# Four linear-attention heads whose instructions are queued one projection earlier in a hybrid block

## The chip, the cores and the metric

The kernel runs on one core of a Trainium2 chip. The metric is the device time of one execution in microseconds (us). Three runs of the kernel before the change gave 1381.58, 1382.93 and 1383.07 us; their median is 1382.93 us.

## The reference, cut to what matters

One encoder layer over 1024 tokens of width 1024, all in float32: a norm, one wide input projection, gated linear attention of four heads in both directions beside a pooling branch, a gated merge, and a feed-forward block. The change lies in the input projection and the attention:

```python
h = rmsnorm(x, norm_mix[l])
proj = h @ w_in[l]
q, k, v, r, lr_f, lr_b, u, g_a, g_b = jnp.split(proj, split_points, axis=-1)
log_a_f = jax.nn.log_sigmoid(lr_f @ w_decay_up_fwd[l] + b_decay_fwd[l]) / GATE_NORMALIZER
log_a_b = ...
o_fwd = gla_chunked(qh, kh, vh, af, include_diag=True)      # per head: 128 keys, 256 values
o_bwd = jnp.flip(gla_chunked(jnp.flip(qh, 2), ..., include_diag=False), 2)
o = o_fwd + o_bwd
o = o * lax.rsqrt(jnp.mean(o * o, axis=-1, keepdims=True) + EPS)
o = o.transpose(0, 2, 1, 3).reshape(bsz, length, GLA_VALUE_DIM) * gla_norm[l]
o = (o * jax.nn.silu(r)).astype(x.dtype)
...
# gla_chunked, per chunk n:  S_n = decay_n * S_(n-1) + k_n^T v_n ;  o_n = (masked q_n k_n^T) v_n + q_n S
```

## The kernel before, in words

Every float32 product is made of three fast ones: both factors are split into a high part (a cast on ScalarE, ACT) and a low part (a subtraction on VectorE, DVE, or GpSimd, POOL), and `mm3` multiplies high by high, low by high and high by low. Weights come from memory as `raw` and are split into `wh` and `wl`; four `raw` buffers serve all weights in turn.

TensorE (PE) runs one long row of these products, 512 wide (`ps`). Counted from the start, the stretch that matters is: Q and K of head 0 (products 136 to 224), values of heads 0 and 1 (to 320), Q and K of head 1 (320 to 416) and of head 2 (416 to 512), values of heads 2 and 3 (512 to 704, by tiles 7, 6, 5 ... 0 of 128 tokens), Q and K of head 3 (704 to 800), then eight tiles of the gate r, `j` = 0 to 7, 48 products each (800 to 1184). Tiles 0 to 2 of r (`BY = 3`) are only kept; from `j` = 3 on each half of a tile also goes through `gated`: Silu on ACT, transposes of the finished attention output on PE (`tp`), and a multiplication on DVE.

Everything else is woven into that row. `pump(dt)` runs after each `mm3`, and gives time to three lists: `pending` (splits of weights for later products), `aside` (`beside(...)`: sums of weight blocks on POOL (`wsum`, stored as `s_out`), and later sums of feature blocks on DVE, one job per `every` units), and `side`, a queue of generators that run one after the other. Each `attention` is such a generator, and `yield t` says how many units of the main row pass before its next piece. It only sets the order in which instructions are issued. Each engine executes its own instructions in that order and waits at each for its inputs.

The pieces of one attention are:
- four gate products `z`, then Abs, Exp and Ln on ACT (a table load lies before Ln, and another before the next Exp); between them the previous head's output is scaled by `normalize` (DVE), and `flush` stores it to memory (`o_out`, issued by SyncE, SP);
- four times: `decay` (scan on DVE), `exponentials` (ACT), `apply_decay` (`ke` on DVE, `qe` on POOL), and two key transposes `kp`, split into `kt`;
- the backward chain, chunks n = 7 to 1: a product `kv` on PE, the state `st` on DVE, and its scaled copies `sb` and `so` on ACT; the next `st` needs `so`;
- the scores `sc`, masked and split into `p`;
- the outputs `op`, n = 0 to 7, each from `p`, the values, `sb` and the forward state `sf`.

Values are kept by `keep_values`, as `vh` (ACT) and `vl` (DVE), a pair of each per tile of tokens for two heads. An attention fetches Q and K as arguments; before its chain it waits, by half a unit at a time, until the dictionary `v_heads` has its head's values, which is filled once all eight tiles are there.

Of the kernel before, what the change touches and what calls it, by code (L numbers as in the profile page):

```python
# [23 lines left out]
HEADS = 4  # L24
# [29 lines left out]
def kernel(  # L54
# [42 lines left out]
    def slot(dtype=F32, shape=(2, HALF), s="slot"):  # L97
        return slots.tile([P, *shape], dtype, tag="slot", name=name(s))
# [90 lines left out]
    def begin(gen, delay=0.0):  # L189
        side.append([gen, delay])  # L190
# [284 lines left out]
    split_pair_weight()  # L475
    for kp in range(2):
        transpose_tile(trs[kp], xn[1], 1, kp)
    pair_v = {}, {}

    def keep_values(vs, t, ps):  # L480
        for v in vs:
            if t // 4 not in v:
                v[t // 4] = slot(F32R, (4, DV), "vh"), slot(F32R, (4, DV), "vl")
        parts = [[part[:, t % 4, :] for part in v[t // 4]] for v in vs]
        halves = [ps[:, h * DV : (h + 1) * DV] for h in range(2)]
        for (hi, _), src in zip(parts, halves):
            nc.scalar.copy(hi, src)
        for (hi, lo), src in zip(parts, halves):
            nc.vector.tensor_tensor(lo, src, as_f32(hi), op=ALU.subtract)

    def pair_products(ts, before=None):
        banks = [bank(ps_mm) for _ in ts]
        for k in range(KT):
            if before:
                before(k)
            for ps, t in zip(banks, ts):
                mm3(ps[:, :], tokens(hT(k, t // 4), t), pair_w[k], k == 0, k == KT - 1)
        for ps, t in zip(banks, ts):
            keep_values(pair_v, t, ps)

    def first_steps(k):
        if k == 2:
# [204 lines left out]
    def prepare_beside(jobs, every, put=PUT, lag=1):  # L707
        aside.append([beside(chain(*jobs), every, put, lag), every])
# [5 lines left out]
            aside.pop(0)  # L714


    v_heads, o_heads, unscaled = {}, {}, []
    HOLD, SCORES = 4.4, 6

    class ValueWeights:  # L720
# [32 lines left out]
        def products(self):  # L753
            while pending:
                pending.pop(0)()
            vs, banks = ({}, {}), {}
            self.split()
            self.split()

            def steps(t, ks):  # L760
                if t not in banks:
                    banks[t] = bank(ps_mm)
                for k in ks:
                    if (t, k) == (0, 6):
                        prepare()
                        credit[0] = 1.0
                    at = self.ORDER.index(k)
                    mm3(banks[t][:, :], tokens(hT(k, t // 4), t), self.parts[k], at == 0, at == KT - 1)
                if ks[-1] == self.ORDER[-1]:
                    keep_values(vs, t, banks[t])  # L770

            early, late = self.ORDER[:6], self.ORDER[6:]
            for ks in (early, late):
                for t in (7, 6):
                    steps(t, ks)
            for t in reversed(range(NT - 2)):
                if t == 2:
                    fetch()
                steps(t, self.ORDER)
            return vs  # L780

    def project_qk(last=False):
        q = slot(s="q")
        k = slot(s="k")
        for dst, scale in ((q, DK**-0.5), (k, 1.0)):
            final = last and dst is k
            w = take(not final)
            if final:
                value_weights[0].splits(2)
            elif last:  # L790
                value_weights.append(ValueWeights())
            for half in range(2):
                ps = feature_major(w, hT, half)
                nc.scalar.activation(dst[:, half, :], ps[:, :], AF.Copy, scale=scale)
        return q, k

    def attention(h, q, k):


        qe, ke = {}, {}  # L800
# [59 lines left out]
        def apply_decay(half, d):  # L860
            if half not in ke:
                ke[half] = slot(s="ke")
            f, e_q, e_k = fac[half, d], qe[half], ke[half]
            f2 = f[:, :8].rearrange("p (n a) -> p n a", a=2)
            nc.vector.tensor_tensor(e_k[:, d, :], zs[half, d][:, :], k[:, half, :], op=ALU.mult)
            nc.gpsimd.tensor_tensor(e_q[:, d, :], e_q[:, d, :], q[:, half, :], op=ALU.mult)
            nc.gpsimd.tensor_tensor(f[:, 8:], f2[:, :, 0], f2[:, :, 1], op=ALU.mult)
# [20 lines left out]
        def advance(old, n, d, kt, dst, ends=False):  # L888

            kv = bank(ps_g, "kv")  # L890
            products(kv[:, :DV], tokens((kt[:, 0, :], kt[:, 1, :]), n), value(n))
            new = s1((DV,), "st")[:, :]
            after = factor(n, d, "after")
            if old is None:
                nc.vector.tensor_scalar(new, kv[:, :DV], after, None, op0=ALU.mult)
            else:
                nc.vector.scalar_tensor_tensor(
                    new, kv[:, :DV], after, old[:, :], op0=ALU.mult, op1=ALU.add
                )
            following = n + 1 if d == 0 else n - 1  # L900
            nc.scalar.activation(dst, new, AF.Copy, scale=factor(following, d, "before"))
            if ends:
                return None
            old = s1((DV,), "so")
            nc.scalar.activation(old[:, :], new, AF.Copy, scale=factor(following, d, "whole"))
            return old
# [17 lines left out]
        exponentials(1, 1)  # L924
        decay(0, 1)
        yield 2
        apply_decay(1, 1)
        yield HOLD - 2
        exponentials(0, 1)
# [10 lines left out]
        kts[0, 1] = transposed_keys(0, 1)  # L940
        exponentials(1, 0)
        yield 2.5
        while h not in v_heads:
            yield 0.5
        v = v_heads[h]

        def value(n):
            return tuple(part[:, n % 4, :] for part in v[n // 4])

        sb = [slot(shape=(4, DV), s="sb") for _ in range(2)]  # L950
        old = None
        for n in range(NT - 1, 0, -1):
            m = n - 1
            old = advance(old, n, 1, kts[n // 4, 1], sb[m // 4][:, m % 4, :], m == 0)
            if n == 7:
                apply_decay(1, 0)
            yield 1.2
            if n == 3:
                kts[0, 0] = transposed_keys(0, 0)
                yield 0.5  # L960
        p = scores(0)
        yield SCORES
        o = [slot(shape=(4, DV), s="o") for _ in range(2)]
        ms = vec(NT, "oms")
        old = sf = None
# [50 lines left out]
    def first_qk():  # L1016
        q, k = slot(s="q"), slot(s="k")
        low_rank(0)
        weights = [take()]
        for half in range(2):  # L1020
            if half:
                finish_side()
                low_rank(1)
                prepare()
            for n, (dst, scale) in enumerate(((q, DK**-0.5), (k, 1.0))):
                if n == len(weights):
                    weights.append(take(ahead=False))
                ps = feature_major(weights[n], hT, half)
                nc.scalar.activation(dst[:, half, :], ps[:, :], AF.Copy, scale=scale)
        return q, k  # L1030

    value_weights = []
    for h in range(HEADS):
        qk = project_qk(h == 2) if h else first_qk()
        begin(attention(h, *qk))
        if h == 0:
            for ts in ((7,), (6,), (5, 4)):
                pair_products(ts)
            v_heads.update(enumerate(pair_v))
            prepare_beside(map(branch_jobs, range(2)), 3.7)  # L1040
        if h == 2:
            v_heads.update(zip((2, 3), value_weights.pop().products()))
            prepare_beside(map(branch_jobs, range(2, 4)), 4)

    class Unit:
# [132 lines left out]
    for j in range(KT):  # L1178
        if 2 <= j <= 4:
            load_o(j - 2)  # L1180
        w = take()
        if j == 6:
            for _ in range(2):
                gunits[0].load()
        if j == 7:
            gates_ahead.step()
        if j < BY:
            whole_r = slot(s="r")
        for half in range(2):
            if j >= BY and not sums_begun and (j > BY or not side):  # L1190
                finish_side()
                finish_beside()
                prepare_beside([feature_jobs(0), feature_jobs(1)], 2.3)
                sums_begun = True
            ps = feature_major(w, hT, half)
            if half == 0:
                flush()
            if j < BY:
                nc.scalar.copy(whole_r[:, half, :], ps[:, :])
                raw_r.append((j, half, whole_r[:, half, :]))  # L1200
            else:
                put_by()
                gated(j, half, ps[:, :])
            if j == KT - 1 and half == 0:
                gates_ahead.step()
# [882 lines left out]
```

## Time and profile before

| what | value |
|---|---|
| median of three runs | 1382.93 us |
| the profiled execution | 1381.07 us, its span 1379.2 us |
| busy time of PE, DVE, ACT, POOL | 1366.3, 836.6, 642.4, 750.6 us |
| granted TensorE clock | 1.00 |

The span is the time from the first to the last recorded instruction; 1.9 us of the execution lie around it. Busy time of an engine counts its instructions and not its waits. In a timeline row stand the start, the duration, the engine, the source line, the operation and its tiles (`out<-in`), and in brackets the idle time before it and who ended that. A row of the waits gives the total, the number and the longest.

### The profile page before, as it was taken

Reading aid. Unit: us, or ns where it says so; the run is one execution under the profiler, and the core shown is the slowest. Engines: PE = TensorE matmul, PEld = TensorE weight load, DVE = VectorE, ACT = ScalarE, POOL = GpSimd, SP = SyncE. Lnnn points to the kernel's source line nnn. Section 1 sums busy time; section 2 is a strip of 40 time slices with the busy share of each in tenths; the row PEclk is TensorE's granted clock in tenths of the full one; section 3 lists DMA queues with packets and bytes.
Section 4 is the critical chain, followed back from the end, with each engine's and each line's share of the span. In section 5 each row is a group of like instructions: output and inputs, shape, how many; then the busy total and the mean of one; then the engine's idle time right before and its main releaser. Section 6 shows DMA issues by size and latency. Waiting matters only on the chain. (4 is left out here: it accounts for less than half of the span.)

```text
span 1379.2 us, 17839 instructions
## 1 busy us (share of the span) xinstructions
PE 1366.3 (99%) x6322; PEld 1135.7 (82%) x6322; DVE 836.6 (61%) x1027; ACT 642.4 (47%) x1170; POOL 750.6 (54%) x554
## 2 busy tenths in 40 slices
PE   9999999999999999999999999999999999999998
PEld 7888888888888888888888888888888888888886
DVE  6364656556935876687884955655655556343375
ACT  7375765664434544554347533333333334444353
POOL 3232704341288546668665276666666667455454
PEclk9999999999999999999999999999999999999999
DMA  6112312342478678996517355555444447985561
GB/s 226 31 54 69 123 40 76 100 138 77 137 221 283 199 225 269 377 392 218 182 62 244 115 176 175 175 176 176 162 130 150 145 139 264 386 305 186 170 214 76
DMA packets 165561, 243.58 MB, mean 177 GB/s; under 512 B 10936, under 2 KB 93920, under 8 KB 165472
## 3 DMA queue, kind: packets, MB, share of 16 engines
q1 hardware_dynamic: 165328, 242.18, 52.4%
q8 instruction: 49, 0.80, 0.2%
q14 instruction: 40, 0.33, 0.1%
q10 hardware_dynamic: 144, 0.26, 0.0%
HBM read 164.55 MB, written 77.86 MB: 176 GB/s over the span
## 5 line engine op out<-in xcount | busy, mean ns | idle before, releaser
L201 POOL TENSOR_TENSOR wl<-fs,wh 128x512 fp32r<-128x512 f32 x120 | 168.0, 1404 | 157.2 <-ACT wh L200 103.3
L273 PE MATMUL ps<-gh,wh 128*128 128x512 f32 x616 | 240.4, 390 | 0.0
L273 PE MATMUL ps<-gl,wh 128*128 128x512 f32 x616 | 239.8, 389 | 0.3 <-DVE gl L1646 0.3
L273 PE MATMUL ps<-gh,wl 128*128 128x512 f32 x616 | 239.7, 389 | 0.0
L201 POOL TENSOR_TENSOR wl<-fraw,wh 128x512 fp32r<-128x512 f32 x90 | 131.6, 1462 | 65.4 <-ACT wh L200 61.8
L273 PE MATMUL ps<-hh,wh 128*128 128x512 f32 x376 | 152.9, 407 | 0.0
L201 POOL TENSOR_TENSOR ol<-gor,oh 128x1024 fp32r<-128x1024 f32 (+1 forms) x42 | 101.6, 2424 | 85.7 <-ACT oh L200 59.6
L273 PE MATMUL ps<-hh,wl 128*128 128x512 f32 x376 | 146.9, 391 | 0.3 <-POOL wl L201 0.3
L273 PE MATMUL ps<-hl,wh 128*128 128x512 f32 x376 | 146.6, 390 | 0.0
L273 PEld LDWEIGHTS ps<-gl,wh 128*128 128x128 f32 x616 | 115.7, 188 | 24.4 <-DVE gl L1646 0.7
L273 PEld LDWEIGHTS ps<-gh,wh 128*128 128x128 f32 x616 | 115.7, 188 | 24.2 <-ACT hb L1665 0.2
L273 PEld LDWEIGHTS ps<-gh,wl 128*128 128x128 f32 x616 | 115.6, 188 | 23.9
L273 PE MATMUL ps<-oh,oh 128*128 128x512 f32 x308 | 119.8, 389 | 0.0
L273 PE MATMUL ps<-ol,oh 128*128 128x512 f32 x308 | 119.8, 389 | 0.0
L273 PE MATMUL ps<-oh,ol 128*128 128x512 f32 x308 | 119.8, 389 | 0.0
L201 POOL TENSOR_TENSOR wl<-raw,wh 128x512 fp32r<-128x512 f32 x38 | 51.3, 1361 | 125.6 <-ACT wh L200 99.8
L201 POOL TENSOR_TENSOR wl<-wraw,wh 128x512 fp32r<-128x512 f32 x56 | 92.8, 1685 | 43.9 <-ACT wh L200 38.2
L201 DVE TENSOR_TENSOR ol<-wor,oh 128x1024 fp32r<-128x1024 f32 (+1 forms) x42 | 62.8, 1506 | 67.8 <-ACT oh L200 55.2
L200 ACT CAST wh<-fs 128x512 fp32r<-128x512 f32 x120 | 73.7, 614 | 26.3 <-DVE fs L1065 25.3
L273 PEld LDWEIGHTS ps<-hh,wl 128*128 128x128 f32 x376 | 70.6, 188 | 15.7 <-POOL wl L201 0.8
L273 PEld LDWEIGHTS ps<-hl,wh 128*128 128x128 f32 x376 | 70.8, 188 | 12.7
L273 PEld LDWEIGHTS ps<-hh,wh 128*128 128x128 f32 x376 | 70.7, 188 | 12.6
(279 smaller groups left out, 3045.7 us busy)
## 6 DMA issues: line engine op xcount, KB each, us to landing
fraw<-in_w_ffn_in_dram SPq DMA_DIRECT2D x44, 512.0 KB, 6.9
gor<-g_out SPq DMA_DIRECT2D x35, 512.0 KB, 4.7
g_out<-s SPq DMA_DIRECT2D x44, 256.0 KB, 2.4
raw<-in_w_in_dram SPq DMA_DIRECT2D x40, 256.0 KB, 5.8
fraw<-in_w_in_dram SPq DMA_DIRECT2D x20, 512.0 KB, 6.7
wor<-t_out SPq DMA_DIRECT2D x20, 512.0 KB, 4.6
g_out<-g SPq DMA_DIRECT2D x33, 256.0 KB, 2.4
x<-in_x_dram SPq DMA_DIRECT2D x16, 512.0 KB, 4.4
```

The source lines that it names most:

```text
L200: nc.scalar.copy(hi, src)
L201: eng.tensor_tensor(lo, src, as_f32(hi), op=ALU.subtract)
L273: nc.tensor.matmul(ps, a[i], b[j], start=first and n == 0, stop=last and n == 2, skip_group_check=onto)
```

## The change

Three things change. The attention of head h + 1 is put into the side queue right behind the projection of head h, so ahead of the projection of its own Q and K. It asks for Q and K in front of its first `apply_decay`, and for the values of each chunk when it comes to that chunk. And the sums of feature blocks are spaced by 2.8 units and no longer 2.3; they begin at r tile 3 if the side queue is empty by then.

```diff
-    pair_v = {}, {}
-    def keep_values(vs, t, ps):
+    v_slots, v_tiles, qk_heads = [{} for _ in range(HEADS)], [set() for _ in range(HEADS)], {}
+    def keep_values(heads, t, ps):
+        vs = [v_slots[h] for h in heads]
...
+        for h in heads:
+            v_tiles[h].add(t)
...
-    def project_qk(last=False):
+    def project_qk(h, last=False):
...
-        return q, k
-    def attention(h, q, k):
+        qk_heads[h] = q, k
+    def attention(h):
...
         exponentials(1, 1)
         decay(0, 1)
         yield 2
+        while h not in qk_heads:
+            yield 0.5
+        q, k = qk_heads[h]
         apply_decay(1, 1)
...
-        while h not in v_heads:
-            yield 0.5
-        v = v_heads[h]
...
         for n in range(NT - 1, 0, -1):
             m = n - 1
+            while n not in v_tiles[h]:
+                yield 0.5
             old = advance(old, n, 1, kts[n // 4, 1], ...)
...
         p = scores(0)
         yield SCORES
+        while 0 not in v_tiles[h]:
+            yield 0.5
...
     for h in range(HEADS):
-        qk = project_qk(h == 2) if h else first_qk()
-        begin(attention(h, *qk))
+        if h:
+            project_qk(h, h == 2)
+        else:
+            first_qk()
+            begin(attention(0))
+        if h < HEADS - 1:
+            begin(attention(h + 1))
...
-                prepare_beside([feature_jobs(0), feature_jobs(1)], 2.3)
+                prepare_beside([feature_jobs(0), feature_jobs(1)], 2.8)
```

Every engine has as many instructions as before. The order differs only between product 398 and product 1184 of the main row (in the profile before, 125.9 to about 380 us). In products of that row, attention 1's pieces come 15 sooner; attention 2's gate products and transposes 15, and its chain, scores and outputs 24 sooner; attention 3's gate products 48, its last output 45 sooner (929, before 974). The feature sums begin at product 944 (`j` = 3) and no longer at 992.

ACT near the end of attention 2's backward chain, before (`st_442`, `st_447` and `st_451` are its last three states, `q_416` is a projection's output, `p_454` the high part of the scores):

```order
L905 ACTIVATE so_443_2355<-st_442_2352,fac_401_2172 128x256
L200 CAST kt_445_2365<-kp_444_2360 128x512
L901 ACTIVATE sb_421_2280<-st_447_2372,fac_401_2172 128x256
L905 ACTIVATE so_448_2375<-st_447_2372,fac_401_2172 128x256
L794 ACTIVATE q_416_2270<-ps_420_2276 128x512
L901 ACTIVATE sb_421_2280<-st_451_2389,fac_401_2172 128x256
L200 CAST p_454_2405<-sc_453_2396 128x512
```

After (`st_431`, `st_436` and `st_444` are the last three; `vh_388` and `vh_390` are tile 0 of the values of heads 2 and 3):

```order
L907 ACTIVATE so_432_2308<-st_431_2305,fac_400_2152 128x256
L200 CAST kt_434_2318<-kp_433_2313 128x512
L903 ACTIVATE sb_412_2237<-st_436_2328,fac_400_2152 128x256
L907 ACTIVATE so_437_2331<-st_436_2328,fac_400_2152 128x256
L490 CAST vh_388_2102<-ps_411_2233 128x256
L490 CAST vh_390_2104<-ps_411_2233 128x256
L903 ACTIVATE sb_412_2237<-st_444_2351,fac_400_2152 128x256
L200 CAST p_447_2367<-sc_446_2358 128x512
```

The copy of `q` has left the chain, and the pair of value casts has come into it, ahead of the last state.

SP around the stores of head 2's output, before (`raw_529` and `raw_530` are the weights of r tile 1):

```order
L677 DMA s_out6_541<-wsum_439_2344 128x512
L677 DMA s_out3_539<-wsum_439_2344 128x512
L560 DMA o_out2_563<-o_456_2429 128x1024
L560 DMA o_out2_563<-o_457_2430 128x1024
L208 DMA raw_529_2779<-in_w_in_dram 128x4x128
L208 DMA raw_530_2781<-in_w_in_dram 128x4x128
L677 DMA s_out5_540<-wsum_510_2657 128x512
L677 DMA s_out7_542<-wsum_510_2657 128x512
```

After (the same weights are `raw_519` and `raw_520`, those of r tile 0 `raw_500` and `raw_501`):

```order
L208 DMA raw_500_2586<-in_w_in_dram 128x4x128
L208 DMA raw_501_2588<-in_w_in_dram 128x4x128
L563 DMA o_out2_563<-o_455_2402 128x1024
L563 DMA o_out2_563<-o_456_2403 128x1024
L680 DMA s_out5_540<-wsum_454_2393 128x512
L680 DMA s_out7_542<-wsum_454_2393 128x512
L597 DMA wsum_517_2694<-in_w_branch_gla_dram 128x2x512
L597 DMA wsum_518_2695<-in_w_branch_gla_dram 128x2x512
L208 DMA raw_519_2704<-in_w_in_dram 128x4x128
L208 DMA raw_520_2706<-in_w_in_dram 128x4x128
```

The stores of head 2's output are now ahead of two stores and two loads of the weight sums, and all of these are ahead of the weights of r tile 1.

PE at the last outputs of attention 3, before (`op_635` is n = 5, `op_649` n = 6; `ps_648` is r tile 3, and `tp` are the transposes for the first gated output):

```order
L979 MATMUL op_635_3225<-sf_631_3209,qe_535_2801 128x256
L1155 MATMUL tp_641_3245<-ident_80,ol_550_2898 128x128 x4
L1155 MATMUL tp_645_3255<-ident_80,ol_592_3069 128x128 x4
L273 MATMUL ps_648_3263<-hh_76_494,wh_564_2946 128x512
L273 MATMUL ps_648_3263<-hl_77_495,wh_564_2946 128x512
L273 MATMUL ps_648_3263<-hh_76_494,wl_565_2947 128x512
L273 MATMUL op_649_3267<-vh_329_1800,p_616_3150 128x256
L273 MATMUL op_649_3267<-vl_330_1801,p_616_3150 128x256
L273 MATMUL op_649_3267<-vh_329_1800,p_617_3151 128x256
```

After (`op_626` is n = 5, `op_631` n = 6; `ps_625` is r tile 2):

```order
L984 MATMUL op_626_3162<-sf_621_3144,qe_526_2735 128x256
L273 MATMUL ps_625_3158<-hh_76_494,wh_548_2858 128x512
L273 MATMUL ps_625_3158<-hl_77_495,wh_548_2858 128x512
L273 MATMUL ps_625_3158<-hh_76_494,wl_549_2859 128x512
L273 MATMUL op_631_3183<-vh_339_1828,p_606_3084 128x256
L273 MATMUL op_631_3183<-vl_340_1829,p_606_3084 128x256
L273 MATMUL op_631_3183<-vh_339_1828,p_607_3085 128x256
L984 MATMUL op_631_3183<-sb_551_2863,qe_526_2735 128x256
```

No gated output lies among attention 3's outputs any more; they end in r tile 2.

More of the change, by code (lines that the diff above doesn't have):

```diff
@@ L498, in pair_products @@
         for ps, t in zip(banks, ts):
-            keep_values(pair_v, t, ps)
+            keep_values((0, 1), t, ps)
     def first_steps(k):
@@ L714, in finish_beside @@
             aside.pop(0)
-    v_heads, o_heads, unscaled = {}, {}, []
+    o_heads, unscaled = {}, []
     HOLD, SCORES = 4.4, 6
@@ L755, in products @@
                 pending.pop(0)()
-            vs, banks = ({}, {}), {}
+            banks = {}
             self.split()
@@ L769, in steps @@
                 if ks[-1] == self.ORDER[-1]:
-                    keep_values(vs, t, banks[t])
+                    keep_values((2, 3), t, banks[t])
             early, late = self.ORDER[:6], self.ORDER[6:]
@@ L779, in products @@
                 steps(t, self.ORDER)
-            return vs
-    def project_qk(last=False):
+    def project_qk(h, last=False):
         q = slot(s="q")
@@ L942, in attention @@
         yield 2.5
-        while h not in v_heads:
-            yield 0.5
-        v = v_heads[h]
         def value(n):
-            return tuple(part[:, n % 4, :] for part in v[n // 4])
+            return tuple(part[:, n % 4, :] for part in v_slots[h][n // 4])
         sb = [slot(shape=(4, DV), s="sb") for _ in range(2)]
@@ L1029, in first_qk @@
                 nc.scalar.activation(dst[:, half, :], ps[:, :], AF.Copy, scale=scale)
-        return q, k
+        qk_heads[0] = q, k
     value_weights = []
     for h in range(HEADS):
-        qk = project_qk(h == 2) if h else first_qk()
-        begin(attention(h, *qk))
+        if h:
[5 more added lines that the diff above has]
+            begin(attention(h + 1))
         if h == 0:
@@ L1038 @@
                 pair_products(ts)
-            v_heads.update(enumerate(pair_v))
             prepare_beside(map(branch_jobs, range(2)), 3.7)
         if h == 2:
-            v_heads.update(zip((2, 3), value_weights.pop().products()))
+            value_weights.pop().products()
             prepare_beside(map(branch_jobs, range(2, 4)), 4)
```

## The prediction

> **What bounds the kernel now.** I read the page's busy times first, then the windows over the part of the program that the new order touches, then who waits for whom on TensorE in 120 to 380 us.
>
> ```profile
> PE 1366.3 (99%) x6322; PEld 1135.7 (82%) x6322; DVE 836.6 (61%) x1027; ACT 642.4 (47%) x1170; POOL 750.6 (54%) x554
> 160.00:200.00 40.00, 39.13 (x218) 33.46 (x217) 20.22 (x43) 23.53 (x62) 8.08 (x9) 1.00 0.00 1
> 200.00:240.00 40.00, 39.45 (x200) 32.68 (x199) 25.98 (x54) 24.29 (x54) 14.00 (x13) 1.00 0.33 99
> 280.00:320.00 40.00, 39.37 (x223) 33.81 (x222) 21.18 (x38) 25.15 (x61) 16.98 (x16) 1.00 0.38 114
> 320.00:340.00 20.00, 18.33 (x98) 15.50 (x96) 13.62 (x24) 8.87 (x19) 5.17 (x3) 1.00 0.24 72
> 340.00:380.00 40.00, 40.00 (x196) 33.37 (x195) 35.01 (x32) 15.64 (x22) 9.65 (x6) 1.00 0.39 127
> PE op L979 <- ACT sf L901: 2.1, 2, 1.7
> PE op L273 <- DVE p L201: 0.7, 3, 0.2
> ```
>
> The columns of a window are its length, then busy time of PE, PEld, DVE, ACT and POOL. PE is full almost everywhere and does the same instructions after the change (the same 5923 rows in both listings), so only its waits can move the time. In the four windows that miss anything it misses 0.87 + 0.55 + 0.63 + 1.67 = 3.7 us. Most of it hangs on two tiles: `p`, which ends the chain from the key-value products to the scores, and `sf`, the running state. This caps the gain at about 3.7 us by the records; the modelled ends of matmuls hide part of a wait (at 324.14 to 326.08 below, 1.82 us by starts against 1.67), so I allow up to 6. There is no such cap on a loss. I cost each attention by one question: how late is `p` when PE comes to it? Where PE stands there already, each us by which the chain is longer relative to PE is a us of the kernel.
>
> **Attention 2, the largest term.** The price of a step on PE, and the chain from kv(7) to `p`:
>
> ```profile
> 327.32 0.40 PE L273 MATMUL ps<-hh,wh 128*128 128x512 f32 x1
> ...
> 329.82 0.39 PE L273 MATMUL ps<-hh,wl 128*128 128x512 f32 x1
> 218.26 0.69 DVE L201 TENSOR_TENSOR kt<-kp,kt 128x512 fp32r<-128x512 f32 x1 [1.16 <-ACT kt L200]
> 221.44 0.28 PE L273 MATMUL kv<-vh,kt 128*128 128x256 f32 x1
> 223.88 0.60 ACT L200 CAST wh<-raw 128x512 fp32r<-128x512 f32 x1
> 224.38 0.64 ACT L487 CAST vh<-ps 128x256 fp32r<-128x256 f32 x2
> 225.06 0.75 DVE L489 TENSOR_TENSOR vl<-ps,vh 128x256 fp32r<-128x256 f32 x2 [1.74 <-ACT vh L487]
> 225.73 0.47 DVE L895 TENSOR_SCALAR st<-kv,fac 128x256 f32<-128x256 f32 x1
> 226.72 0.49 ACT L905 ACTIVATE so<-st,fac 128x256 f32<-128x256 f32 x1
> 227.24 0.48 DVE L897 SCALAR_TENSOR_TENSOR st<-kv,fac,so 128x256 f32<-128x256 f32 x1 [0.44 <-ACT so L905]
> 238.10 0.39 PE L273 MATMUL op<-vh,p 128*128 128x256 f32 x1 [0.22 <-DVE p L201]
> ```
>
> Eleven 512-wide products take 329.82 - 327.32 = 2.50 us, 0.227 each. The listings put attention 2's gate products and key transposes 15 products sooner (3.4 us), but its kv products 24 sooner (5.45 us), since kv(7) no longer stands behind the value product of tile 0. Its DVE and ACT work keeps its length. So PE reaches kv(7) 2.04 us sooner relative to the work that must be ready. Two things are given back. One pair of `vl` subtractions (225.73 - 225.06 = 0.67) now falls into the 1.16 us in which DVE stood before `kt`. And no `wh` cast stands any more between the last exponentials and the `vh` for which DVE waited (224.38 - 223.88 = 0.50). The first `st` came 225.73 - 221.44 = 4.29 us behind kv(7); after, 4.29 + 2.04 - 0.67 - 0.50 = 5.16. That is 0.87 worse.
>
> The chain itself also gets longer: tile 0's values are now split inside it. Normally the next `st` starts 0.52 us after the start of `so` (226.72, 227.24). With a pair of `vh` on ACT and a pair of `vl` on DVE in between, it starts after about 0.49 + 0.64 + 0.04 + 0.67 = 1.84, less 0.1 of overlap on ACT: 1.25 more. Single weight casts inside the chain cost nothing, as ACT has a gap there each step (0.55 us, quoted below). PE already waits at 238.10, so both go on the path: **+2.1 us**. Ends: +0.4 (a third of the insertion, no worse lag) to +3.1 (a weight piece, whose cast now stands inside the chain, comes late too).
>
> **Attention 1.**
>
> ```profile
> 147.96 0.62 ACT L200 CAST wh<-raw 128x512 fp32r<-128x512 f32 x1 [2.01 <-DMA raw<-in_w_in_dram]
> 149.90 0.60 ACT L855 ACTIVATE qe<-z 128x512 f32<-128x512 f32 x1
> 155.84 0.61 ACT L794 ACTIVATE k<-ps 128x512 f32<-128x512 f32 x1
> 156.33 1.15 ACT L200 CAST wh<-raw 128x512 fp32r<-128x512 f32 x2
> 162.98 0.51 ACT L901 ACTIVATE sb<-st,fac 128x256 f32<-128x256 f32 x1 [0.55 <-DVE st L897]
> 152.34 1.23 DVE L835 TENSOR_TENSOR_SCAN z<-carry,la 128x512 f32<-128x512 bf16 x1
> 157.90 1.83 DVE L835 TENSOR_TENSOR_SCAN z<-carry,la 128x512 f32<-128x512 bf16 x1
> 160.90 0.47 DVE L895 TENSOR_SCALAR st<-kv,fac 128x256 f32<-128x256 f32 x1
> 157.35 1.28 POOL L866 TENSOR_TENSOR qe<-qe,q 128x512 f32<-128x512 f32 x1
> 173.32 0.38 PE L273 MATMUL op<-vh,p 128*128 128x256 f32 x1 [0.22 <-DVE p L201]
> ```
>
> Before its first exponentials (149.90) ACT stood 2.01 us for a raw weight piece. Two of the value-weight casts ahead of them now stand behind them. The piece that the new order still needs is loaded into a buffer that comes free late, and `o_out` is stored ahead of it, so I count less than half of the 2.01: 0.85 sooner at `st`. Against that, a `k` copy and two `wh` casts now stand together inside the chain: 0.49 + 1.15 - 0.1 of overlap = 1.54 in a gap of 0.55, 0.97 more. The values of tiles 7 and 6 of the next heads, and no longer three tiles, are split beside its outputs; the smaller of the two `sf` waits (2.1 - 1.7 = 0.4) should go. **-0.85 + 0.97 - 0.4 = -0.3 us**; ends -1.4 (all 2.01 gained, by which the chain's 0.7 of waits are gone) to +1.0 (nothing gained).
>
> The scan alone takes 1.23 us, beside a POOL multiplication 1.83. The Trainium skill ("SBUF — State Buffer", Who interferes with whom) says that a DVE instruction with two SBUF inputs and a GpSimd one that reads SBUF exclude each other for a whole instruction. The row agrees: the scan ends 0.13 us sooner than POOL's end at 158.63 plus 1.23. My term keeps one such meeting, 0.60. By the rule the worst is a full POOL instruction, 1.28, and the sum would be 0.7 higher; with no meeting it would be 0.6 lower.
>
> **Attention 3: a stall goes, a load comes late.**
>
> ```profile
> 324.02 0.28 PE L273 MATMUL op<-vl,p 128*128 128x256 f32 x1
> 324.14 0.28 PE L273 MATMUL op<-vh,p 128*128 128x256 f32 x1
> 326.08 0.70 PE L979 MATMUL op<-sf,qe 128*128 128x256 f32 x2 [1.67 <-ACT sf L901]
> 321.73 1.28 ACT L1152 ACT_TABLE_LOAD   x1
> ...
> 273.93 1.34 SPq L208 DMA_DIRECT2D raw<-in_w_in_dram  x2
> 278.57 0.62 ACT L200 CAST wh<-raw 128x512 fp32r<-128x512 f32 x1 [3.42 <-DMA raw<-in_w_in_dram]
> 146.94 0.90 SPq L677 DMA_DIRECT2D s_out<-wsum  x2
> 256.37 0.94 SPq L594 DMA_DIRECT2D wsum<-in_w_branch_gla_dram  x2
> wsum<-in_w_branch_gla_dram SPq DMA_DIRECT2D x8, 512.0 KB, 4.4
> s_out<-wsum SPq DMA_DIRECT2D x16, 256.0 KB, 3.7
> GB/s 226 31 54 69 123 40 76 100 138 77 137 221 283 199 225 269 377 392 218 182 62 244 115 176 175 175 176 176 162 130 150 145 139 264 386 305 186 170 214 76
> ```
>
> The longest wait is at 326.08: the last `sf` stands behind the Silu table load (321.73), two Silu passes and DVE's gating of the first finished tile. After the change attention 3 ends before that output, so this goes: 326.08 - 324.14 - 0.12 (the step from one 256-wide matmul to the next, 324.02 to 324.14) = 1.82 us. What is late next is its `p`.
>
> There SP's order counts. Before, the raw weights of the next tile of r were issued right behind the `o_out` stores, and ACT, with a `wh` cast ahead of the first exponentials, waited 3.42 us for them (278.57). Now two `s_out` stores and two `wsum` loads stand in between: 0.90 + 0.94 = 1.84 us of issue at least, and at most the transfer of 2 x 256 + 2 x 512 KB = 1.5 MB at the fullest slice's 392 GB/s, 3.9 us. I take 2.5, nearer to the issue times. The gate products stand 87 products before the key transposes instead of 84, which gives 0.7 back. So the chain is 1.8 us later where PE waits already: **+1.8 - 1.8 = 0.0 us**; ends -2.5 (the loads come in time) to +1.4.
>
> **The rest.** Feature sums start 48 products (10.9 us) sooner and 2.8 apart instead of 2.3. I cost this at nothing: PE missed nothing in 340 to 380, where they ran beside the gating with DVE 35 of 40 us busy; wider spacing loads DVE less. Without that cover it costs what late gating cost at 326.08, 1.8 us. The new waits for Q, K and value tiles are on the issuing program, not on an engine, and queue nothing.
>
> **Sum:** 2.1 - 0.3 + 0.0 = +1.8 us, or 1381.07 + 1.8 = 1382.9 on the profiled execution, whose time is 1.9 under the median of 1382.93. On the median: **1384.8 us**, 0.13% slower. A measurement of this kernel tells about 0.2% (2.8 us) from no change, so the likeliest result is one that can't be told apart.
>
> **Rivals.**
> - *The chains gain what the earlier start promises* (faster). Attention 3's weights come in time: -2.5; attention 1 gains its 2.01: -1.4; attention 2 pays only its low end: +0.4. Sum -3.5: 1379.4 us. For it: two of the ACT waits above are for loads, and a queue of attentions that is never empty hides them. Against: SP's new order puts more in front of the load, not less. It decides itself by whether ACT's wait at the first `wh` behind the last logarithms of attention 3 is under 1.5 us. Chance 0.16.
> - *SP's order takes the place of the removed stall* (slower). In attention 3 the full 3.9 us come through, +1.4; attention 1 gains nothing, +1.0; attention 2 +2.1. Sum +4.5: 1387.4 us. For it: ACT waited 3.42 there with an empty queue in front. It decides from about 3.4 us of added landing time, where the sum passes 2.8 with attention 1 at +0.2. Chance 0.38.
> - *Nothing but PE's fixed work counts*, and the waits merely move: within 1 us of 1382.9. For it: PE is 99% busy. It lies inside the forecast's band, whose chance is 0.46.
>
> **How the numbers follow.** Forecast and band within 0.2%: 0.46; slower 0.38; faster 0.16. The ends of the terms add to -3.5 and +5.5; all at one end together is unlikely, so the range for 8 in 10 goes from -2.6 to +4.8: 1380.3 to 1387.7 us.
>
> **What would show it.** Right: in attention 2, `st` of kv(7) comes about 5.2 us behind kv(7), one step of the kv chain is 1.2 us longer beside a `vh` pair, and PE's wait for `p` there grows to some 3 us. In attention 3, no wait at the last `sf`; ACT waits over 5 us at the `wh` ahead of the first exponentials, and PE at `p` for about 3 us. In attention 1, `st` 3.2 us behind kv(7). Wrong: `st` of attention 2 less than 4.3 us behind kv(7); or `raw` of attention 3 landing as soon behind the `o_out` store as before; or a new wait of PE after 340 us, which would charge the feature sums.

## The result and the profile after

| kernel | median | lowest to highest | ratio to before, 95% interval |
|---|---|---|---|
| before | 1382.91 us (6 runs) | 1381.58 to 1383.49 | |
| after | 1389.07 us (6 runs) | 1388.15 to 1389.50 | 1.0045 [1.0032, 1.0058] |

The change makes the kernel 6.2 us slower. The sign of the forecast was right, its size was not: 1384.8 was forecast, and 1389.07 lies above the range. The profiled execution took 1388.15 us, its span 1386.1; against the profile before that is 7.1 us more. One run of `e1_late_store` (3134.2 us) and one of `e8_tiles_only` (2311.5 us), both below, took far longer than all the others; the ratios leave them out, and they move the medians by under 0.1 us.

The page of the kernel after, its busy times; then the windows of the kernel after that answer to those of before, and three short ones:

```profile
PE 1367.5 (99%) x6322; PEld 1136.6 (82%) x6322; DVE 837.0 (60%) x1027; ACT 642.2 (46%) x1170; POOL 752.4 (54%) x554
```

```profile
200.00:240.00 40.00, 36.90 (x191) 30.08 (x191) 25.20 (x49) 23.41 (x55) 13.94 (x13) 1.00 0.26 71
...
275.00:280.00 5.00, 0.75 (x4) 0.29 (x2) 0.00 (x0) 2.96 (x5) 1.26 (x1) 0.83 0.93 298
280.00:285.00 5.00, 4.20 (x12) 3.52 (x13) 4.18 (x6) 3.45 (x11) 4.28 (x4) 0.50 0.00 0
285.00:290.00 5.00, 5.00 (x28) 4.16 (x27) 4.40 (x7) 1.54 (x3) 5.00 (x6) 0.99 0.14 52
...
320.00:340.00 20.00, 20.00 (x101) 16.89 (x100) 12.48 (x22) 7.94 (x17) 7.87 (x4) 1.00 0.11 30
340.00:380.00 40.00, 40.00 (x199) 33.43 (x198) 32.50 (x29) 15.81 (x23) 9.80 (x7) 1.00 0.36 119
```

PE's work is the same. The window 320 to 340, where before the last `sf` was late, is now full (20.00, before 18.33). But 200 to 240 misses 3.1 us where it missed 0.55, and from 275 to 280 PE does almost nothing: 0.75 of 5 us, with DVE at 0.00 and the DMA engines at 0.93. Who was waited for, in the kernel after, from 120 to 400 us:

```profile
PE kp L885 <- DVE ke L867: 6.1, 2, 5.0
PE op L273 <- ACT p L200: 1.1, 1, 1.1
PE sc L915 <- DVE st L899: 0.5, 2, 0.3
PE op L273 <- DVE p L201: 0.5, 2, 0.2
PE kv L273 <- DVE st L897: 0.4, 1, 0.4
```

The waits for `sf` (2.1 before) are gone, and a single one of 5.0 us has come, in front of the key transposes. To see where the 7.1 us lie, the same products are looked up in both timelines. Before (products 800, 992 and 1183 of the main row):

```profile
262.35 0.39 PE L273 MATMUL ps<-hh,wl 128*128 128x512 f32 x1
...
330.50 0.40 PE L273 MATMUL ps<-hh,wl 128*128 128x512 f32 x1
...
379.73 0.39 PE L273 MATMUL ps<-hl,wh 128*128 128x512 f32 x1
```

After, the same three:

```profile
265.85 0.39 PE L273 MATMUL ps<-hh,wl 128*128 128x512 f32 x1
...
337.36 0.39 PE L273 MATMUL ps<-hh,wl 128*128 128x512 f32 x1
...
386.58 0.39 PE L273 MATMUL ps<-hl,wh 128*128 128x512 f32 x1
```

Product 800 starts 3.50 us later, of which 0.9 is only the four `z` of attention 3, which now stand ahead of it: 2.6 are lost in attentions 1 and 2. At product 992 attention 3 is done in both kernels, and the delay is 6.86: another 4.3 is lost in attention 3. At 1183 it is 6.85, so the feature sums lose nothing. The 2.6 splits by summing how far each matmul's start lies beyond its usual step: attention 1 from 6.93 us to 6.36 (-0.6), attention 2 from 6.25 to 9.34 (+3.1); the same count gives attention 3 8.04 and 12.37 (+4.3).

**Attention 3.** How its chain starts, before:

```profile
263.26 0.39 PE L806 MATMUL z<-lrT,up 128*128 128x512 f32 x1
...
267.08 6.41 DVE L1000 TENSOR_SCALAR o<-o,ors 128x256 f32<-128x256 f32 x8
...
270.33 3.51 SPq L560 DMA_DIRECT2D o_out<-o  x2
...
280.51 0.60 ACT L855 ACTIVATE qe<-z 128x512 f32<-128x512 f32 x1
```

And after:

```profile
254.94 0.40 PE L808 MATMUL z<-lrT,up 128*128 128x512 f32 x1
...
259.46 7.25 DVE L1005 TENSOR_SCALAR o<-o,ors 128x256 f32<-128x256 f32 x8
...
262.44 4.64 SPq L563 DMA_DIRECT2D o_out<-o  x2
267.19 1.20 SPq L680 DMA_DIRECT2D s_out<-wsum  x2
268.48 2.36 SPq L597 DMA_DIRECT2D wsum<-in_w_branch_gla_dram  x2
270.94 0.98 SPq L208 DMA_DIRECT2D raw<-in_w_in_dram  x2
...
277.01 0.62 ACT L200 CAST wh<-raw 128x512 fp32r<-128x512 f32 x1 [9.85 <-DMA raw<-in_w_in_dram]
278.94 0.60 ACT L857 ACTIVATE qe<-z 128x512 f32<-128x512 f32 x1
280.06 0.69 DVE L867 TENSOR_TENSOR ke<-z,k 128x512 f32<-128x512 f32 x1 [8.03 <-ACT z L858]
280.80 1.12 PE L885 MATMUL kp<-ident,ke 128*128 128x128 f32 x4 [5.05 <-DVE ke L867]
```

The chain of the stall reads from the bottom up. PE waits 5.05 us for `ke`, DVE 8.03 for the exponentials, ACT 9.85 at a `wh` cast for raw weights, and these are issued by SP only once the stores of `o_out`, two `s_out` and two `wsum` are through; the first of them waits for DVE's scaling of the output. The first exponentials came 280.51 - 263.26 = 17.25 us behind the first `z` before, and 278.94 - 254.94 = 24.00 after: 6.75 us later. By parts, each measured from `z`: the `o_out` stores are out at 12.14 and no longer 10.58 (+1.56; the scaling takes 7.25 and no longer 6.41, and begins later), behind them the two stores and two loads take 270.94 - 267.08 = 3.86, where the weights followed at once before (273.93 - 273.84 = 0.09), so +3.77, and from issue to cast it is 6.07, before 4.64 (+1.43). The three make the 6.75 but for rounding.

**Attention 2**, kernel after:

```profile
214.95 0.66 PE L885 MATMUL kp<-ident,ke 128*128 128x128 f32 x4 [1.02 <-DVE ke L867]
216.83 0.28 PE L273 MATMUL kv<-vh,kt 128*128 128x256 f32 x1
...
221.68 0.47 DVE L897 TENSOR_SCALAR st<-kv,fac 128x256 f32<-128x256 f32 x1
...
230.12 0.47 DVE L899 SCALAR_TENSOR_TENSOR st<-kv,fac,so 128x256 f32<-128x256 f32 x1
...
232.10 0.76 DVE L492 TENSOR_TENSOR vl<-ps,vh 128x256 fp32r<-128x256 f32 x2 [1.50 <-ACT vh L490]
232.77 0.47 DVE L899 SCALAR_TENSOR_TENSOR st<-kv,fac,so 128x256 f32<-128x256 f32 x1
234.52 0.39 PE L273 MATMUL op<-vh,p 128*128 128x256 f32 x1 [1.13 <-ACT p L200]
```

The last step of the backward chain, with tile 0's values split inside it, takes 232.77 - 230.12 = 2.65 us. A plain step takes 1.46 in both kernels, so 1.19 is added.

### The profile page after: what moved, and what is told of

It is laid out like the page before. It is cut to its first block, busy times and chain, and to the rows that moved or that the text cites. A ratio compares the mean times of both kernels' runs of the same rounds, so it can differ in the third digit from the quotient of the medians.

```text
span 1386.1 us, 17826 instructions
## 1 busy us (share of the span) xinstructions
PE 1367.5 (99%) x6322; PEld 1136.6 (82%) x6322; DVE 837.0 (60%) x1027; ACT 642.2 (46%) x1170; POOL 752.4 (54%) x554
## 5 line engine op out<-in xcount | busy, mean ns | idle before, releaser
L201 POOL TENSOR_TENSOR wl<-raw,wh 128x512 fp32r<-128x512 f32 x38 | 55.4, 1472 | 116.1 <-ACT wh L200 98.7
```

Of the source, the lines that this page charges most:

```text
L201: eng.tensor_tensor(lo, src, as_f32(hi), op=ALU.subtract)
```

## Experiments

Each kernel was timed against the kernel before, in five rounds; the ratios are to before. "The place" of an attention is the product of the main row at which its first `z` is issued: attention 3 stands at 803 before and at 755 after.

**1. The store moved behind the load** (`e1_late_store`). Head 2's scaled output is kept back, and stored in r tile 0 only once the weights of r tile 1 are asked for.

```diff
-        flush()
+        if h < HEADS - 1:
+            flush()
```

> Only the two stores of head 2's output (o_out2) move: they are issued in the first tile of r, behind the weights of r tile 1, instead of ahead of them. Theory (the load behind the stores is the loss of attention 3): ACT's wait at the first wh cast behind the logarithms falls from 9.85 us to under 4, PE's 5.0 us wait for ke is gone, the granted clock stays at 1.00 through 275 to 290 us, and the time falls by about 7 us, to 1382. Rival (attention 3's own DVE and ACT work, begun 10.9 us sooner, is what comes late): ke still waits about 5 us and the time stays within 1 us of 1389.

Measured: 1383.94 us, 1.0008 [0.9999, 1.0017], 5.1 under after. SP and ACT in its timeline:

```profile
239.01 25.08 SPq L680 DMA_DIRECT2D s_out<-wsum  x2
...
265.23 0.97 SPq L208 DMA_DIRECT2D raw<-in_w_in_dram  x2
...
267.55 0.99 SPq L563 DMA_DIRECT2D o_out<-o  x2
...
271.69 0.62 ACT L200 CAST wh<-raw 128x512 fp32r<-128x512 f32 x1 [4.36 <-DMA raw<-in_w_in_dram]
```

The weights are asked for 5.7 us sooner (265.23 against 270.94), the cast starts 5.3 sooner, and the 5.05 us wait of PE is gone. Most of what the change lost hangs on this one store in front of this one load. The run came 1.9 us above what my theory gave. It counted on 7 us, but the wait that went was 5.05, and the half clock behind that wait gives nothing back, as experiment 2 shows. ACT still waits 4.36 us, because the load still stands behind two stores and two loads of weight sums: the second `s_out` is issued only when POOL has finished its sum (the row at 239.01 ends at 264.09), and the weights follow at 265.23. In attention 3 PE waits only 0.3, 0.2 and 0.2 us, for `kt`, the state and `p`.

**2. Is it the clock?** (`e2_fill`). In 280 to 285 us PE ran at half clock (0.50 above), right behind its idle 5 us. If that costs time, work put into the idle stretch wins it back. 22 products that nothing reads are put ahead of attention 3's first key transposes.

```diff
+        if h == HEADS - 1:
+            spare = bank(ps_g, "spare")
+            for _ in range(22):
+                nc.tensor.matmul(spare[:, :], hT(0, 0)[0][:, :P], hT(0, 0)[0][:, :], start=True, stop=True)
```

> Ahead of attention 3's first key transposes PE gets 22 products of 512 columns whose result nobody reads (5.0 us), so that it works during the 5.05 us wait for ke; nothing else changes. Theory (after the idle PE runs at half its clock for some 5 us, which costs about 1.9 us by the starts of its products): no clock under 0.95 in 275 to 290 us, and about 2 us less, 1387. Rival (the low clock has another reason, or costs nothing): the same time, 1389, or more by what of the 22 products does not fit into the wait.

Measured: 1388.65 us, 1.0045 [1.0032, 1.0059], as the kernel after. Its window behind the filled stretch:

```profile
280.00:285.00 5.00, 4.84 (x26) 3.78 (x25) 4.00 (x6) 3.43 (x9) 4.53 (x4) 1.00 0.00 0
```

The clock is at 1.00, where the kernel after had 0.50, and the 5 us wait is gone, and the time is the same. The half clock was real but free: PE, faster here, only reaches the next waits for DVE sooner (0.4 us for `kt`, 0.2 each for `ke`, the state and `p`, where the kernel after has none behind its 5.0). My theory that it cost some 2 us falls.

**3. Values whole again** (`e3_whole_values`). The attention waits for all eight tiles of values ahead of its chain, as before; the rest of the change stays.

```diff
+        while len(v_tiles[h]) < NT:
+            yield 0.5
         for n in range(NT - 1, 0, -1):
             m = n - 1
-            while n not in v_tiles[h]:
-                yield 0.5
```

> Every attention waits, as before the change, for all eight value tiles of its head ahead of its first kv; the rest is as after the change. Only attention 2 meets this wait: its chain goes back by 24 products. Theory (its added 3.1 us come from PE reaching kv(7) sooner than the work ahead of st, and from the split of tile 0 inside the chain): attention 2's wait at p goes from 1.1 + 0.2 us to under 0.6, the sc and kv waits there go too, and the time falls by 2 to 2.5 us, to 1386.8; PE's wait for ke in attention 2 (1.0 us) stays. Rival (the loss of attention 2 is only this wait for ke, which the scans beside POOL cause): within 0.6 us of 1389.

Measured: 1378.22 us (1378.10 to 1379.46), 0.9971 [0.9959, 0.9982]: 10.9 under after and 4.3 under before, far better than either theory had it. Timeline and, in a fence of its own, who PE waits for from 120 to 400 us:

```profile
257.80 1.01 SPq L208 DMA_DIRECT2D raw<-in_w_in_dram  x2
...
262.76 2.18 DVE L1005 TENSOR_SCALAR o<-o,ors 128x256 f32<-128x256 f32 x8
263.92 1.39 SPq L563 DMA_DIRECT2D o_out<-o  x2
...
269.30 1.16 ACT L200 CAST wh<-raw 128x512 fp32r<-128x512 f32 x2
```

```profile
PE kp L885 <- DVE ke L867: 1.0, 1, 1.0
PE ps L273 <- POOL wl L201: 0.6, 1, 0.6
PE sc L915 <- DVE st L899: 0.2, 1, 0.2
PE op L273 <- DVE p L201: 0.2, 1, 0.2
```

What I had overlooked is in the order. With whole values attention 2 ends at product 776 and no longer at 752, so attention 3, behind it in the queue, begins at 779 and no longer at 755. The store of the output that it scales then stands, in the order of issue, behind the load of the weights, which has its place at product 800. The load goes first, at 257.80, the store at 263.92, and the cast ahead of the exponentials finds the weights there, with no wait in its row. All waits of attention 3 are gone.

**4. Both** (`e4_whole_late`): the edits of 1 and 3 together.

> Both of the edits together: o_out2 stored behind the weights of r tile 1, and the chain held until all eight value tiles are there. If the two losses are separate, the gains add: 7 + 2.3 = 9.3 us less than after, 1379.8, which is 3 us under the kernel before. Rival (one loss hides the other, since a later attention 2 also delays attention 3): about 1382.

Measured: 1378.11 us, 0.9971 [0.9960, 0.9982], as 3. Where attention 3 stands at 779, the store is already behind the load, and moving it does nothing.

**5 and 6. The parts of the change by themselves.** `e5_spacing` is 3 with the feature sums 2.3 units apart again, so the kernel before with the attentions queued sooner and nothing else. `e8_tiles_only` is the kernel before with values asked for tile by tile and nothing else (its attention takes Q and K as arguments again, and is begun behind them).

```diff
-                prepare_beside([feature_jobs(0), feature_jobs(1)], 2.8)
+                prepare_beside([feature_jobs(0), feature_jobs(1)], 2.3)
```

And `e8_tiles_only` against the kernel after:

```diff
-        if h:
-            project_qk(h, h == 2)
-        else:
-            first_qk()
-            begin(attention(0))
-        if h < HEADS - 1:
-            begin(attention(h + 1))
+        qk = project_qk(h == 2) if h else first_qk()
+        begin(attention(h, *qk))
...
-                prepare_beside([feature_jobs(0), feature_jobs(1)], 2.8)
+                prepare_beside([feature_jobs(0), feature_jobs(1)], 2.3)
```

> As the run with whole values, but the feature sums stay 2.3 units apart. Theory (PE has no wait there, so neither the spacing nor the earlier start counts): within 1 us of that run's 1378.2. Rival (the sums, denser beside the gating, make DVE late): a new PE wait between 310 and 380 us and over 1379.5.

> The kernel before with one part of the change: values are asked for tile by tile. Only attention 2 moves: its chain, scores and outputs stand 9 products sooner (kv from 698, not 707), and tile 0 is split inside the chain. Theory (PE reaches the chain sooner than DVE and ACT are ready, and the split lengthens it by 1.25): PE's waits in attention 2 grow by 1.5 to 3 us, 1384.6. Rival (an earlier chain is an earlier p): 1381 or less.

Measured: `e5_spacing` 1379.43 us (1378.15 to 1379.63), 0.9975 [0.9965, 0.9985]; `e8_tiles_only` 1384.50, 1.0011 [1.0002, 1.0020]. Alone, the earlier queue wins 3.2 us and the values by tile lose 1.9; added up that is -1.3, and together they lose 6.2. So 7.5 us come only from both, by way of attention 3's place. The spacing doesn't matter here. `e5_spacing` lies 1.2 over 3, a little more than expected, but the runs of both fall on two levels of some 1378.2 and 1379.5, and the profile of 3 is on the lower, that of `e5_spacing` on the upper. What the second trace has more of waits (0.4 for `ke`, 0.3 for `kt`, 0.3 for the state) lies in attention 1, before 190 us, far ahead of the sums; from product 577 to 1183 both take 187.4 us. What makes the levels is told below.

**7 and 8. Attention 3's place by itself.** `e6_att3_back` is after with attention 3 begun behind its own Q and K, at 803. `e9_delay3` is after with attention 3 resting 8 units at the head of the queue, at 779; values come by tile in both.

```diff
-        if h < HEADS - 1:
+        if h < HEADS - 2:
             begin(attention(h + 1))
+        if h == HEADS - 1:
+            begin(attention(h))
```

```diff
-            begin(attention(h + 1))
+            begin(attention(h + 1), 8 if h == 2 else 0)
```

> As after the change, but attention 3 is queued behind the projection of its own Q and K, as before (gate products at 803). Theory (the losses add up by attention: -0.6 in attention 1, +3.1 in attention 2, +4.3 in attention 3): what is left is +2.5 on the kernel before, 1385.1, and the load that attention 3 waits for comes as before (some 3.4 us of ACT's wait). Rival (everything is attention 3's load): 1382.6 or less.

> As after the change, values still tile by tile, but attention 3 rests for 8 units at the head of the queue: its gate products stand at 779 and no longer at 755. By the listings the load of r tile 1's weights is then issued ahead of the stores of head 2's output, and the casts of these weights come without a wait. Theory (attention 3's loss is its place against that load, not its being queued early, and not the values by tile): its waits vanish as in the run with whole values, -3.3 us instead of +4.3, attention 2 keeps its +3.1, and the time is 1381.4 to 1381.9. Rival (attention 3 gains in the other run only because attention 2 ends without a loss): 1385 or more.

Measured: `e6_att3_back` 1385.08 us, 1.0017 [1.0008, 1.0026]; `e9_delay3` 1381.07, 0.9991 [0.9982, 1.0000]. `e9_delay3` in the timeline:

```profile
264.19 0.97 SPq L208 DMA_DIRECT2D raw<-in_w_in_dram  x2
267.56 1.39 SPq L563 DMA_DIRECT2D o_out<-o  x2
...
272.95 1.16 ACT L200 CAST wh<-raw 128x512 fp32r<-128x512 f32 x2
```

Between it and the kernel after nothing differs but 24 products of attention 3's place, and it is 8.0 us faster by the medians (7.6 from product 577 to 1183 of the two traces; up to 577 their order is the same): load, then store, and a cast without a wait. With the place at 803 the waits of before come back, the one for the last `sf` among them, and 4.0 of the 8.0 are lost again. The three places with the same values give 1389.1 (755), 1381.1 (779) and 1385.1 (803). Against 3 (1378.22), `e9_delay3` shows what the values by tile cost outside attention 3's load: 2.9 us by the medians.

**9. A version that beats both** (`e7_delay2`): 3, with attention 2 resting 5 units, so that PE doesn't reach its key transposes too soon (the 1.0 at `kp` above).

```diff
-            begin(attention(h + 1))
+            begin(attention(h + 1), 5 if h == 1 else 0)
```

> As the run with whole values, but attention 2 rests for 5 units at the head of the queue, so its gate products stand at 593 as before; its chain, which waits for the values anyway, stays at 707, and attention 3 stays at 779. Theory (PE's wait of 1.0 us for ke in attention 2 comes from its z to kp work being begun while that of attention 1's outputs and the value splits still run): that wait shrinks to under 0.3, 1377.4. Rival (it has a fixed length, whenever it begins): 1378.2, and an interval that holds that run.

Measured: 1377.43 us (1377.28 to 1378.78), 0.9965 [0.9953, 0.9978]. It has the lowest median, 5.2 under before (1382.65 beside it), and of PE's waits for `ke` from 120 to 400 us only this row is left:

```profile
PE kp L885 <- DVE ke L867: 0.4, 1, 0.4
```

The row is not attention 2's: it lies before 190 us, in attention 1, where four other profiles have the same 0.4 (those in which a scan of DVE takes some 2.4 us, below). In attention 2 the wait of 1.0 is gone, as the theory had it. The intervals don't tell this kernel from 3, but from product 577 to 1183 its trace takes 186.5 us against 187.4.

## Why the prediction was wrong

**The step that failed is the late load of attention 3.** It was put at 2.5 us, with 1.84 (issue times) and 3.9 (one transfer) as bounds; measured are 6.75. The two bounds were alternatives of one thing, the two stores and two loads in between, and these alone took 3.77. Left out were the store at their head, which waits for DVE's scaling and came 1.56 later behind `z`, and the landing of the weights, 1.43 longer behind what was issued ahead of them.

The scaling is itself held up, which the prediction did not look at: its eight multiplications take 2.18 us where POOL is idle (experiment 3), but in the kernel after five of them start beside an instruction of POOL and end 0.15 us behind it, which makes 7.25. Before, it was four of them, and 6.41.

With 6.75 in the place of 2.5 the prediction's own sum reads 6.75 - 0.7 - 1.8 = +4.3 for attention 3 (measured +4.3), and 2.1 - 0.3 + 4.3 = +6.1 in all. That 6.2 was measured between the medians is in part luck, since attention 2 cost 1.0 more than forecast and attention 1 0.3 less: the parts that were measured add up to 6.8, and the profiles lie 6.85 apart at product 1183. The other steps there hold: the 0.7 given back, and the 1.8 of the last `sf` gone (20.00 of 20 us busy in 320 to 340).

Also wrong was where PE would pay: at `kp`, ahead of the chain, and not at `p`. The wait for the exponentials was longer than all that PE had to do until it needed `ke`. The sign that was to tell, ACT waiting over 5 us at the `wh`, came with 9.85. Four of the prediction's own sums are a little off (1.22 and not 1.25 for the insertion, 0.99 and not 0.97 in attention 1, 4.0 and not 3.9 for the transfer, 1384.7 and not 1384.8 at the end); none of them moves anything by more than 0.1 us.

**The range** was too narrow for the same reason: its slow end charged 3.9 us for the load. The rival in which SP's order takes the place of the removed stall named the mechanism, and experiments 1 and 8 (`e9_delay3`) show it: put the load ahead of the store, by either of two edits, and PE's 5 us wait is gone. Its price, 1387.4, came from the same bound.

**Attention 2** (+2.1 forecast, +3.1 measured) went by the mechanism described, with one wait more. The insertion of tile 0's values added 1.19 (1.25 forecast). The first `st` came 221.68 - 216.83 = 4.85 behind kv(7) against 5.16 forecast, but PE had also been held at `kp`, for 1.02, which the prediction had not seen: 5.87 without that hold. PE paid in five places (1.02 + 0.41 + 0.30 + 1.13 + 0.23 = 3.1, where the records before have 0.55), not by one wait of 3 us at `p`.

**Attention 1** (-0.3 forecast, -0.6 measured): the wait for raw weights stayed, 2.00 us, and moved from a `wh` to a `wv` cast; the waits for `sf` went, as forecast, and the waits left are 0.24 at `sc` and 0.23 at `p`. The first `st` came 3.45 us behind kv(7), 3.2 was forecast. That the three parts of this term are each right wasn't tried.

**The rest** (0 forecast): right. Between products 992 and 1183 the delay stays at 6.86 and 6.85, and in 340 to 380 PE misses nothing.

**The contended scan.** The prediction weighed the Trainium skill's rule ("SBUF — State Buffer", Who interferes with whom) that a DVE instruction with two SBUF inputs and a GpSimd one that reads SBUF exclude each other for a whole instruction, and put it at 0.6 to 0.7 us either way. Two kernels in whose traces DVE and POOL begin within 0.1 us of each other in attention 1 bear it out. After:

```profile
148.35 1.23 DVE L837 TENSOR_TENSOR_SCAN z<-carry,la 128x512 f32<-128x512 bf16 x1
148.44 2.22 POOL L868 TENSOR_TENSOR qe<-qe,q 128x512 f32<-128x512 f32 x1
```

And `e5_spacing`:

```profile
148.26 2.40 DVE L837 TENSOR_TENSOR_SCAN z<-carry,la 128x512 f32<-128x512 bf16 x1
148.29 1.28 POOL L868 TENSOR_TENSOR qe<-qe,q 128x512 f32<-128x512 f32 x1
```

One of the two keeps its own time (1.23 or 1.28) and the other pays about 1 us more. So such a meeting is worth nothing or about 1.2 us to DVE, close to the whole POOL instruction of 1.28 that the prediction named as the worst.

The profiles put the two levels of the runs down to this toss. Nine profiles are of kernels with the earlier queue, and up to product 577 every engine has the same instructions in the same order in all nine. In four of them POOL paid (after, experiments 1, 2 and 3), and product 577 starts at 189.4 to 189.5 us. In five DVE paid (4, 5, 7, 8 and 9; 2.29 to 2.40), and it starts at 190.5 to 190.9. The four lie at the lower end of their kernels' runs, the five at the upper: 1378.28 in 3, 1379.40 in 4. The kernel before has the same meeting, with one of POOL's sums: its profile had POOL pay, as the one after, so that these two can be compared.

**What stays open.** No edit held one of the two engines back, so the link from this toss to the levels rests on nine profiles that all agree, and not on an experiment. What decides the toss from run to run isn't shown either. Nor was it tried what the load costs when the scaling is kept apart from POOL's instructions.

## What to carry to other kernels

A queue that issues in order turns any move of a store into a move of every load behind it: when a piece of work moves, look up which loads with a fixed place in the program it passes, and what the store waits for, and price such a load by the whole way (the store's own wait, everything issued between, and the landing), since these add up and are no bounds of one another. Ask of each part of a change what it does to the place of the next piece in the queue: two parts that are worth -3.2 and +1.9 us alone made +6.2 together, and 24 products of place were worth 8.0 by the medians. And try the parts apart before judging the whole, since half of this change, with one rest in the queue, is 5.2 us faster than the kernel before.

## What the runs showed of the hardware

- In 5.05 us of idle PE the granted clock fell. By windows of 0.2 us it fell at 278.3, some 2.5 us after PE's last product had ended (275.75), and was back at 285.1, 4.3 us after PE had begun again; in between it stood at 0.50 for 6.8 us. The Trainium skill ("TensorE: Matmul & The Clock Gate", What's actually happening) says that the gate halves the clock after an idle window of about 3.4 us, and releases it after such a window of work. The half and the release agree; the fall came sooner than after 3.4 us of idle PE. What I had not expected is that it cost nothing: with the clock held at 1.00 by unread products (experiment 2) the kernel took 1388.65 us against 1389.07.
- Which of DVE and POOL is held at such a meeting shows in the recorded starts only when they lie apart. In the eleven profiles here (before and `e8_tiles_only` have a sum in the place of `qe`), POOL paid in the four in which DVE's start stands 0.05 to 0.09 us ahead, and DVE in the three in which POOL's stands ahead. In the other four DVE's stands 0.00 to 0.04 ahead, and DVE paid in three of them, POOL in one.
- A multiplication of DVE by one value per row (128x256, 0.34 us) that started with or behind an instruction of POOL, while that ran, ended 0.15 us behind it: so in all nine such cases at the scaling of head 2's output, five in the kernel after and four before.
